# Strassen's seven products for blocks 6 to 17 of the Down products, in a decoder trunk on one Trainium2 core

## The chip, the core and the metric

The kernel runs on one core of one Trainium2 chip. The metric is the device time of one execution in microseconds; of several runs the median counts. Five engines work side by side, each with its own queue in fixed order: PE (TensorE, matmuls; its weight loads are listed as PEld), DVE (VectorE), ACT (ScalarE), POOL (GpSimd) and SP, which here only issues DMAs. POOL issues DMAs too, those that add what they load to what already lies in the tile.

## The reference

Two layers, each with two feed-forward parts around a mixer. Sequence 512, model width 1024, hidden width 2816 (22 blocks of 128), all in f32:

```python
def swiglu(x, w1, w3, w2):
    return (jax.nn.silu(x @ w1) * (x @ w3)) @ w2
...
    for l in range(DEPTH):
        h = x + 0.5 * swiglu(rms_norm(x, ffn1_norm[l]), ffn1_w1[l], ffn1_w3[l], ffn1_w2[l])
...
        h = h + y @ w_out[l]
        h = h + 0.5 * swiglu(rms_norm(h, ffn2_norm[l]), ffn2_w1[l], ffn2_w3[l], ffn2_w2[l])
        x = rms_norm(h, final_norm[l])
```

`x @ w1` and `x @ w3` are called Up here, the last product, with `w2`, Down. The mixer between the parts (convolution, window attention, attention to a memory) is not touched.

## The kernel before, in words

The activations lie transposed: h is [128, 8, 512], eight output blocks d of 128 channels by 512 positions. Each f32 product is made of three matmuls (mm3, lines 177 to 180): an operand is split into a high part that the matmul takes exactly and a low rest, and high x high, high x low and low x high are summed in PSUM. A split (line 145) is a copy on ACT that rounds (hi), then a subtraction on DVE (lo).

A feed-forward part (ffn, line 422) forms the hidden blocks f and folds them into h in four groups, QUARTERS (line 28): blocks 0 to 5, 6 to 11, 12 to 17, 18 to 21. Blocks 0 to 3 of Up are plain products, the others come in pairs from up_pair (line 358), by Strassen's seven products of quarters: two halves of the model width by two blocks, times two halves of the positions. Each of its seven units of weights (1024 columns, raw, a sum of raws, or X, which a load and an adding DMA on POOL's queue make, line 366) serves 24 matmuls of 256 columns. Their sums leave the four banks po and pt through ACT (part, lines 392 to 405) and DVE (add, line 386); then silu (line 414), the gating product (line 415) and the split of the gated blocks into ghi and glo (lines 416 to 419).

Behind a group's pairs, and one more pair made ahead for the next group, comes its Down (lines 488 to 506): for each of eight d a load of the group's columns of w2 into raw, one split, nf x 3 matmuls of 512 columns into one bank mm, and one update of h on DVE (line 506).

The order on each queue is set when the program is built: a scheduler with a model of the costs takes, for each engine, the earliest instruction in program order that its model has ready, and gives out the buffers in the same way; issue_after adds an edge. The chip then keeps that order. The buffers that matter: raw 3, aux (X) 3, whi and wlo 4 of 1024 columns each, ghi and glo 4 of two blocks each, g 2, u 1, part ("sq") 2, banks mm 3 and cf 1; mm() (line 86) takes cf every fourth time.

Of the kernel before, what the change touches and what calls it, by code (L numbers as in the profile page):

```python
# [10 lines left out]
F32 = mybir.dt.float32  # L11
F32R = mybir.dt.float32r
I32 = mybir.dt.int32
AF = mybir.ActivationFunctionType
# [4 lines left out]
P = 128  # L19
# [5 lines left out]
NT = S // P  # L25
FF = 2816
NF = FF // P
QUARTERS = ((0, 6), (6, 6), (12, 6), (18, 4))
CC = 3
TAPS = 31  # L30
PAD = TAPS - 1
# [34 lines left out]
def trunk(ctx: ExitStack, tc: tile.TileContext, xT, memT, pos, w1a, w3a, w2a, w1b, w3b, w2b,  # L66
# [19 lines left out]
    def mm():  # L86

        turn[0] += 1
        return bank([P, S], "mm" if turn[0] % 4 else "cf")
# [55 lines left out]
    def split(hi, lo, x, on):  # L145
        a = A.activation(hi, x, AF.Copy)  # L146
        return a, on.tensor_tensor(out=lo, in0=x, in1=hi.bitcast(F32), op=ALU.subtract)  # L147
# [34 lines left out]
    def at(p, *idx):  # L182
        return tuple(x[idx] for x in p)

    def blk(k, n=P):
        return slice(k * n, (k + 1) * n)
# [158 lines left out]
    def gated_pair():  # L345

        return (gp.tile([P, 2, S], F32R, tag="ghi", name="ghi"), gp.tile([P, 2, S], F32R, tag="glo", name="glo"))

    def gated():
        p = gated_pair()  # L350
        return [at(p, ALL, i, ALL) for i in range(2)]
# [6 lines left out]
    def up_pair(l, w13, f, M):  # L358
# [50 lines left out]
        for i in range(2):  # L409
            product(zv[i][:, x1], w, i, 4)  # L410
            add(to[i][:, 1, x0], zv[i][:, x1], part[i][:, x1])
        out = gated()
        for n, sign in enumerate((1.0, -1.0)):
            A.activation(u[:, n], u[:, n], AF.Silu, scale=sign)
        M.gated = V.tensor_tensor(out=g, in0=g, in1=u, op=ALU.mult)
        for n, sign in enumerate((1.0, -1.0)):
            hi, lo = out[n]
            A.activation(hi, g[:, n], AF.Copy, scale=sign)
            V.scalar_tensor_tensor(out=lo, in0=g[:, n], scalar=sign, in1=hi.bitcast(F32), op0=ALU.mult, op1=ALU.subtract)
        return out  # L420

    def ffn(l, w13, w2, x, sums, factors, last, at_product, aside=None, closing=None):

# [51 lines left out]
                    M.first()  # L475
        M.rest()
        hold.clear()
        for q, (f0, nf) in enumerate(QUARTERS):
            ahead = 2 if q + 1 < len(QUARTERS) else 0
            for f in range(f0, f0 + nf + ahead, 2):  # L480
                if f not in g:
                    g[f], g[f + 1] = up_pair(l, w13, f, M)
                    if f == PLAIN:
                        with tc.issue_after(M.gated.ins):
                            rescale = after()
            begun = []

            def begin(d):
# [770 lines left out]
```

## Time and profile before

| | us |
|---|---|
| median of three runs | 1771.48 (1764.68 to 1775.84) |
| the profiled execution | 1765.18, span 1763.4 |
| granted TensorE clock | 0.998 |

A page of the profile gives each engine's busy time over the span, the chain of waits that ended last, and groups of instructions by line, operation and shape. PE durations overlap, so the spacing of their starts says what a matmul costs.

### The profile page before, as it was taken

Reading aid. Unit: us, or ns where it says so; the run is one execution under the profiler, and the core shown is the slowest. Engines: PE = TensorE matmul, PEld = TensorE weight load, DVE = VectorE, ACT = ScalarE, POOL = GpSimd, SP = SyncE. Lnnn points to the kernel's source line nnn. Section 1 sums busy time; section 2 is a strip of 40 time slices with the busy share of each in tenths; the row PEclk is TensorE's granted clock in tenths of the full one; section 3 lists DMA queues with packets and bytes.
Section 4 is the critical chain, followed back from the end, with each engine's and each line's share of the span. In section 5 each row is a group of like instructions: output and inputs, shape, how many; then the busy total and the mean of one; then the engine's idle time right before and its main releaser. Section 6 shows DMA issues by size and latency. Waiting matters only on the chain.

```text
span 1763.4 us, 28084 instructions
## 1 busy us (share of the span) xinstructions
PE 1746.2 (99%) x11004; PEld 1575.8 (89%) x11004; DVE 1281.0 (73%) x1898; ACT 901.2 (51%) x1373; POOL 196.7 (11%) x220
## 2 busy tenths in 40 slices
PE   8999999999999999999999999999999999999998
PEld 6989999988888989898989898999888889998987
DVE  6969666589877857575678786666898777665756
ACT  6646444365765535353655453444567655353533
POOL 1001000016221000000010010000251310000000
PEclk9999999999999999999999999999999999999999
DMA  9556655267247546465566465642661666574622
GB/s 275 129 162 176 178 131 149 64 173 162 73 98 177 139 137 176 131 167 138 152 146 168 143 177 146 168 132 73 169 163 44 141 150 172 136 185 115 170 82 84
DMA packets 97205, 253.60 MB, mean 144 GB/s; under 512 B 9904, under 2 KB 16304, under 8 KB 97072
## 3 DMA queue, kind: packets, MB, share of 16 engines
q1 hardware_dynamic: 78064, 190.45, 35.6%
q0 software_dynamic: 19008, 61.35, 19.5%
q8 instruction: 86, 1.41, 0.3%
q14 instruction: 47, 0.39, 0.1%
HBM read 249.67 MB, written 2.10 MB: 143 GB/s over the span
## 4 chain that ended last, share of the span: by engine, by line
PE 89%; DVE 7%; DMA 2%; ACT 1%; issue 1%; SPq 0%; DVEq 0%; ACTq 0%
PE mm L178 13%; PE mm L179 12%; PE mm L180 12%; PE po L180 9%; PE po L178 9%; PE po L179 9%; PE pt L178 6%; PE pt L180 6%; PE pt L179 6%; DVE there L993 4%; PE po L870 1%; DMA raw<-in_wconv 1%; PE pt L859 1%; PE mm L818 1%; PE cf L178 0%
## 5 line engine op out<-in xcount | busy, mean ns | idle before, releaser
L146 ACT ACTIVATE whi<-raw 128x1024 fp32r<-128x1024 f32 (+3 forms) x346 | 326.1, 946 | 438.9 <-PE mm L179 222.6
L147 DVE TENSOR_TENSOR wlo<-raw,whi 128x1024 fp32r<-128x1024 f32 (+3 forms) x346 | 376.5, 1090 | 119.4 <-ACT whi L146 118.2
L179 PE MATMUL mm<-glo,whi 128*128 128x512 f32 (+1 forms) x752 | 292.3, 389 | 0.0
L178 PE MATMUL mm<-ghi,whi 128*128 128x512 f32 (+1 forms) x752 | 291.9, 390 | 0.0
L180 PE MATMUL mm<-ghi,wlo 128*128 128x512 f32 (+1 forms) x734 | 285.0, 388 | 0.0
L180 PE MATMUL po<-mh,wlo 128*128 128x256 f32 x864 | 244.7, 283 | 0.0
L179 PE MATMUL po<-ml,whi 128*128 128x256 f32 x864 | 244.7, 283 | 0.0
L178 PE MATMUL po<-mh,whi 128*128 128x256 f32 x864 | 244.6, 283 | 0.0
L180 PE MATMUL pt<-xhi,wlo 128*128 128x256 f32 x864 | 244.2, 283 | 0.0
L179 PE MATMUL pt<-xlo,whi 128*128 128x256 f32 x864 | 244.1, 283 | 0.0
L178 PE MATMUL pt<-xhi,whi 128*128 128x256 f32 x864 | 243.5, 283 | 0.0
L506 DVE SCALAR_TENSOR_TENSOR h<-mm,h 128x512 f32<-128x512 f32 x126 | 86.5, 689 | 129.5 <-PE mm L180 129.5
L178 PEld LDWEIGHTS mm<-ghi,whi 128*128 128x128 f32 x752 | 141.4, 188 | 28.8 <-DVE h L506 1.2
L179 PEld LDWEIGHTS pt<-xlo,whi 128*128 128x128 f32 x864 | 165.9, 192 | 0.8
L178 PEld LDWEIGHTS po<-mh,whi 128*128 128x128 f32 x864 | 165.9, 192 | 0.7
L179 PEld LDWEIGHTS po<-ml,whi 128*128 128x128 f32 x864 | 165.9, 192 | 0.6
L178 PEld LDWEIGHTS pt<-xhi,whi 128*128 128x128 f32 x864 | 165.3, 192 | 1.0
L179 PEld LDWEIGHTS mm<-glo,whi 128*128 128x128 f32 x752 | 141.4, 188 | 27.6
L180 PEld LDWEIGHTS po<-mh,wlo 128*128 128x128 f32 x864 | 165.9, 192 | 0.0
L180 PEld LDWEIGHTS pt<-xhi,wlo 128*128 128x128 f32 x864 | 165.8, 192 | 0.0
L180 PEld LDWEIGHTS mm<-ghi,wlo 128*128 128x128 f32 x734 | 137.9, 188 | 28.3
L993 DVE SCALAR_TENSOR_TENSOR there<-ypad,par,there 128x512 f32<-128x512 f32 x180 | 136.9, 784 | 1.1
(334 smaller groups left out, 3323.0 us busy)
## 6 DMA issues: line engine op xcount, KB each, us to landing
raw<-in_w2a SPq DMA_DIRECT2D x48, 384.0 KB, 3.6
raw<-in_w2b SPq DMA_DIRECT2D x48, 384.0 KB, 3.5
raw<-in_w1b SPq DMA_DIRECT2D x26, 512.0 KB, 3.6
raw<-in_w3b SPq DMA_DIRECT2D x26, 512.0 KB, 4.0
raw<-in_w1a SPq DMA_DIRECT2D x25, 512.0 KB, 3.7
raw<-in_w3a SPq DMA_DIRECT2D x25, 512.0 KB, 3.9
wsum<-in_w1a SPq DMA_DIRECT2D x18, 512.0 KB, 4.4
wsum<-in_w3a SPq DMA_DIRECT2D x18, 512.0 KB, 4.3
```

The costliest lines, as they stand in the source:

```text
L146: a = A.activation(hi, x, AF.Copy)
L147: return a, on.tensor_tensor(out=lo, in0=x, in1=hi.bitcast(F32), op=ALU.subtract)
L178: T.matmul(ps, a[0], b[0], start=first, stop=False, **more)
L179: T.matmul(ps, a[0], b[1], start=False, stop=False, **more)
L180: tail[0] = T.matmul(ps, a[1], b[0], start=False, stop=last, **more)
L506: added = V.scalar_tensor_tensor(out=h[:, d, :], in0=ps, scalar=0.5, in1=h[:, d, :], op0=ALU.mult, op1=ALU.add)
L818: tail[0] = T.matmul(pp[i][:, z, :], q, k, start=not masked, stop=True, skip_group_check=True)
L859: tail[0] = T.transpose(pt[:, i, j, :], pr[:, i, blk(j)], ident)
L870: tail[0] = T.matmul(po[:, 2 * c + i, :], ptb[:, i, j, :], v, start=(j == 0), stop=(j == nk - 1))
L993: V.scalar_tensor_tensor(out=cv[:, c, :], in0=ypad[:, c, j : j + S], scalar=conv_w[:, c, j : j + 1], in1=cv[:, c, :], op0=ALU.mult, op1=AL ...
```

## The change

GROUPS replaces QUARTERS: blocks 0 to 5 and 18 to 21 stay as they are, and 6 to 17 form three groups of four. For a group of four, down_four is called twice, for outputs 0 to 3 and 4 to 7. It takes the four blocks by four outputs of w2 and the four blocks by 512 positions of the gated values as two by two quarters, and forms seven products of quarters. A product is, for each of two outputs i, two blocks k by three matmuls of 256 columns.

The seven operands on the side of the gated values are made per pair in gated_parts: the split of the gated pair, four additions on POOL in place in g, and the split of the result into a second pair of ghi and glo. Since those four tiles then hold only one group, the gated pair made ahead waits in the list waiting, and gone() splits it when the next pair is about to be emitted.

The seven operands on the side of the weights are made in down_four: two loads of 1024 columns into raw, two sums xs on POOL in aux tiles (`xs[:, i]`), two additions in place on DVE per raw, and splits of 512 columns (half_unit). Sums of products leave PSUM through ACT into part and late, and reach h through POOL (most) or, straight from PSUM, through DVE (more, and one update over two outputs). late has the one buffer that is also u's.

The diff:

```diff
--- before.py
+++ after.py
@@ -25,7 +25,8 @@
 NT = S // P
 FF = 2816
 NF = FF // P
-QUARTERS = ((0, 6), (6, 6), (12, 6), (18, 4))
+GROUPS = ((0, 6), (6, 4), (10, 4), (14, 4), (18, 4))
+SEVEN = range(6, 18)
 CC = 3
 TAPS = 31
 PAD = TAPS - 1
@@ -409,15 +410,104 @@
         for i in range(2):
             product(zv[i][:, x1], w, i, 4)
             add(to[i][:, 1, x0], zv[i][:, x1], part[i][:, x1])
-        out = gated()
         for n, sign in enumerate((1.0, -1.0)):
             A.activation(u[:, n], u[:, n], AF.Silu, scale=sign)
         M.gated = V.tensor_tensor(out=g, in0=g, in1=u, op=ALU.mult)
+        return g
+
+    def split_gated(g):
+
+        out = gated()
         for n, sign in enumerate((1.0, -1.0)):
             hi, lo = out[n]
             A.activation(hi, g[:, n], AF.Copy, scale=sign)
             V.scalar_tensor_tensor(out=lo, in0=g[:, n], scalar=sign, in1=hi.bitcast(F32), op0=ALU.mult, op1=ALU.subtract)
         return out
+
+    T0, T1 = blk(0, QT), blk(1, QT)
+
+    def gated_parts(g, m):
+
+        plain = split_gated(g)
+        (a, b), (c, d) = (((g[:, n, T0]), g[:, n, T1]) for n in range(2))
+        G.tensor_tensor(out=d, in0=b, in1=d, op=ALU.add)
+        G.tensor_tensor(out=b, in0=a, in1=b, op=ALU.subtract)
+        G.tensor_tensor(out=a, in0=d, in1=a, op=ALU.subtract)
+        G.tensor_tensor(out=c, in0=a, in1=c, op=ALU.subtract)
+        p = gated_pair()
+        hi, lo = (x.rearrange("p n s -> p (n s)") for x in p)
+        split(hi, lo, g.rearrange("p n s -> p (n s)"), V)
+        sums = [at(p, ALL, i, ALL) for i in range(2)]
+        for j, z, n, t in ((1, plain, 0, T0), (2, plain, 1, T0), (3, plain, 1, T1), (6, sums, 0, T0), (5, sums, 0, T1), (4, sums, 1, T0), (7, sums, 1, T1)):
+            m.setdefault(j, []).append(at(z[n], ALL, t))
+
+    def down_four(l, w2, f0, d0, m):
+
+        xs = wst.tile([P, UNIT], F32, tag="aux", name="wsum", bufs=3).rearrange("p (i n k c) -> p i n k c", i=2, n=2, k=2)
+        raw, rows = [], []
+        for i in range(2):
+            r = wst.tile([P, UNIT], F32, tag="raw", name="raw", bufs=3)
+            d = d0 + 2 * i
+            nc.sync.dma_start(r.rearrange("p (d c) -> p d c", d=2), w2[l, d : d + 2, :, f0 * P : f0 * P + 512].rearrange("d p c -> p d c"))
+            v = r.rearrange("p (d k s c) -> p d k s c", d=2, k=2, s=2)
+            raw.append(r[:, 0:512])
+            rows.append(v)
+            G.tensor_tensor(out=xs[:, i], in0=v[:, :, :, 0], in1=v[:, 1].rearrange("p k s c -> p s k c"), op=ALU.add)
+        banks = [mm() for _ in range(4)]
+        xy, zv = banks[:2], banks[2:]
+        part = [tm("part", "sq", 2) for _ in range(2)]
+        late = tmp.tile([P, 2, S], F32, tag="u", name="late", bufs=1)
+
+        def half_unit(x):
+            p = at(pair(), ALL, slice(0, 512))
+            split(p[0], p[1], x, V)
+            return p
+
+        def product(ps, w, block, j, first=False):
+            for k in range(2):
+                mm3(ps, at(w, ALL, blk(block(k))), m[j][k], first and not k, k == 1, skip_group_check=True)
+
+        def more(d, t, ps):
+            V.scalar_tensor_tensor(out=h[:, d, t], in0=ps, scalar=0.5, in1=h[:, d, t], op0=ALU.mult, op1=ALU.add)
+
+        def most(d, t, x, op=ALU.add):
+            G.tensor_tensor(out=h[:, d, t], in0=h[:, d, t], in1=x, op=op)
+
+        for i in range(2):
+            d = d0 + 2 * i
+            w = half_unit(raw[i])
+            product(xy[i][:, T0], w, lambda k: 2 * k, 1, first=True)
+            product(xy[i][:, T1], w, lambda k: 2 * k + 1, 2)
+            A.activation(part[i], xy[i], AF.Copy, scale=0.5)
+            most(d, T0, part[i][:, T0])
+            most(d, T0, part[i][:, T1])
+            v = rows[i][:, 0]
+            V.tensor_tensor(out=v[:, :, 0], in0=v[:, :, 0], in1=xs[:, i, 1], op=ALU.add)
+            V.tensor_tensor(out=v[:, :, 1], in0=v[:, :, 1], in1=v[:, :, 0], op=ALU.add)
+        for i in range(2):
+            w = half_unit(raw[i])
+            product(xy[i][:, T0], w, lambda k: 2 * k, 6)
+            A.activation(late[:, i, T0], xy[i][:, T0], AF.Copy, scale=0.5)
+            product(zv[i][:, T0], w, lambda k: 2 * k + 1, 3, first=True)
+        for i in range(2):
+            d = d0 + 2 * i
+            w = half_unit(xs[:, i].rearrange("p n k c -> p (n k c)"))
+            product(xy[i][:, T0], w, lambda k: 2 + k, 5)
+            A.activation(late[:, i, T1], xy[i][:, T0], AF.Copy, scale=0.5)
+            product(zv[i][:, T1], w, lambda k: k, 7)
+            V.scalar_tensor_tensor(out=h[:, d : d + 2, T1], in0=zv[i].rearrange("p (n t) -> p n t", n=2), scalar=0.5, in1=h[:, d : d + 2, T1],
+                                   op0=ALU.mult, op1=ALU.add)
+            most(d, T1, late[:, i, T1])
+            most(d + 1, T1, late[:, i, T1], ALU.subtract)
+        w = at(pair(), ALL, slice(0, 512))
+        for i in range(2):
+            hi, lo = (x[:, blk(i, QT)].rearrange("p (k c) -> p k c", k=2) for x in w)
+            split(hi, lo, rows[i][:, 1, :, 1], V)
+        for i in range(2):
+            d = d0 + 2 * i
+            product(zv[i][:, T1], w, lambda k: 2 * i + k, 4)
+            more(d + 1, T0, zv[i][:, T1])
+            most(d + 1, T0, late[:, i, T0], ALU.subtract)
 
     def ffn(l, w13, w2, x, sums, factors, last, at_product, aside=None, closing=None):
 
@@ -475,14 +565,33 @@
                     M.first()
         M.rest()
         hold.clear()
-        for q, (f0, nf) in enumerate(QUARTERS):
-            ahead = 2 if q + 1 < len(QUARTERS) else 0
+        waiting, parts, done = [], {}, set(g)
+
+        def gone():
+
+            while waiting:
+                f, z = waiting.pop(0)
+                if f in SEVEN:
+                    gated_parts(z, parts.setdefault((f - 6) // 4, {}))
+                else:
+                    g[f], g[f + 1] = split_gated(z)
+
+        for q, (f0, nf) in enumerate(GROUPS):
+            ahead = 2 if q + 1 < len(GROUPS) else 0
             for f in range(f0, f0 + nf + ahead, 2):
-                if f not in g:
-                    g[f], g[f + 1] = up_pair(l, w13, f, M)
+                if f not in done:
+                    gone()
+                    waiting.append((f, up_pair(l, w13, f, M)))
+                    done.add(f)
                     if f == PLAIN:
                         with tc.issue_after(M.gated.ins):
                             rescale = after()
+            if f0 in SEVEN:
+                for d in (0, 4):
+                    down_four(l, w2, f0, d, parts[q - 1])
+                continue
+            if not ahead:
+                gone()
             begun = []
 
             def begin(d):
```

## The prediction

> **What bounds the kernel now.** I read the page first: its engines, and the chain that ended last.
>
> ```profile
> span 1763.4 us, 28084 instructions
> PE 1746.2 (99%) x11004; PEld 1575.8 (89%) x11004; DVE 1281.0 (73%) x1898; ACT 901.2 (51%) x1373; POOL 196.7 (11%) x220
> PE 89%; DVE 7%; DMA 2%; ACT 1%; issue 1%; SPq 0%; DVEq 0%; ACTq 0%
> ```
>
> TensorE is never without work, and 89% of the chain is its matmuls. Then the windows of one group of the second feed-forward part: three pairs of Up, then the Down products of six blocks.
>
> ```profile
> 651.60:712.10 60.50, 60.50 (x500) 60.22 (x499) 41.51 (x52) 33.32 (x48) 5.18 (x6) 1.00 0.70 178
> 712.10:744.70 32.60, 32.60 (x151) 27.24 (x150) 19.71 (x25) 9.11 (x11) 0.00 (x0) 1.00 0.37 107
> ```
>
> After the window come us, then PE, PEld, DVE, ACT and POOL busy, the clock, the DMA share and GB/s. PE fills both windows, at full clock. So nothing can be won there but matmul time, and every stall that the change brings counts in full. DVE is busy for 69% of Up and 60% of Down; POOL adds nothing in Down. The waits of that Down window say how the splits are placed:
>
> ```profile
> ACT whi L146 <- PE mm L179: 19.2, 7, 3.2
> DVE h L506 <- PE mm L180: 10.5, 7, 2.5
> ```
>
> ACT waits for PE to give a weight buffer back: the splits run ahead of PE as far as four buffers allow.
>
> **The matmuls.** How long a matmul holds PE is read from starts, since the durations overlap. First a run of 256 columns, then the first of a run of 132 of 512 columns and the matmul that follows its last:
>
> ```profile
> 599.72 0.28 PE L180 MATMUL po<-mh,wlo 128*128 128x256 f32 x1
> ...
> 601.52 0.28 PE L180 MATMUL po<-mh,wlo 128*128 128x256 f32 x1
> ...
> 714.84 0.40 PE L178 MATMUL mm<-ghi,whi 128*128 128x512 f32 x1
> ...
> 744.79 0.28 PE L178 MATMUL po<-mh,whi 128*128 128x256 f32 x1
> ```
>
> Between the first two lie 15 starts: 1.80 / 15 = 0.120 us. The others give 29.95 / 132 = 0.227 us. Four blocks times four outputs are 4 x 4 x 3 = 48 matmuls of 512 columns now, 48 x 0.227 = 10.90 us. Seven products of 2 x 2 x 3 are 84 of 256 columns, 84 x 0.120 = 10.08 us. The eighth product saves 12.5% of the columns, but half a matmul costs 0.120 and not 0.1135, so 0.82 us is left. Down_four is called 3 x 2 times in each of four parts: 24 x 0.82 = **19.7 us saved**. That is all the change can win: PE has no idle time in Down to give back.
>
> **What it puts on DVE and ACT.** The spacing of back-to-back DVE instructions:
>
> ```profile
> 666.33 0.68 DVE L386 TENSOR_TENSOR u<-pt,part 128x512 f32<-128x512 f32 x1
> 666.93 0.68 DVE L386 TENSOR_TENSOR raw<-raw 128x512 f32<-128x512 f32 x1
> ...
> 676.70 1.22 DVE L147 TENSOR_TENSOR wlo<-wsum,whi 128x1024 fp32r<-128x1024 f32 x1
> 677.84 0.42 DVE L386 TENSOR_TENSOR u<-part 128x256 f32<-128x256 f32 x1
> 678.17 1.29 DVE L419 SCALAR_TENSOR_TENSOR glo<-g,ghi 128x512 fp32r<-128x512 f32 x2
> ```
>
> That is 0.60 us for 512 elements, 1.14 for 1024 and 0.33 for 256. One down_four holds six splits of 512 and two of 256 (4.26), four adds into raw of 256 (1.32), and out of PSUM two updates of 512 and two of 256 (1.86): 7.4 us in 10.1 us of PE, of which 5.6 have both inputs in SBUF. A pair of blocks adds one split of 1024 (1.14). By itself DVE would still keep up, 74% busy where it was 60%.
>
> ```profile
> L146 ACT ACTIVATE whi<-raw 128x512 fp32r<-128x512 f32 x36 | 21.8, 625 | 29.8 <-issue 16.6 <-PE pt L179 8.3 <-DMA raw<-in_w2b 2.3
> L400 ACT ACTIVATE part<-po 128x256 f32<-128x256 f32 x72 | 27.3, 380 | 71.1 <-PE po L180 70.9 <-PE pt L179 0.2
> ```
>
> ACT gets six copies of 512 and two of 256 for the splits, two of 512 for part, four of 256 for late: 8 x 0.62 + 6 x 0.38 = 7.2 us of 10.1. I take nothing for it; its cover is the 2.9 us left over in each call, and if that is gone, PE waits for the difference.
>
> **What it puts on POOL.** The trace has no add of 256 elements there, but one of 512, and products of 64 and 192:
>
> ```profile
> L1018 POOL TENSOR_TENSOR aux<-there x2: 1256/1258/1259, 480.6 to 1352.3; 128x512 f32<-128x512 f32 x2
> L753 POOL TENSOR_TENSOR uu<-query,sg x32: 320/874/2593, 398.1 to 1292.3; 128x192 f32<-128x192 f32 x16, 128x64 f32<-128x64 f32 x16
> ```
>
> From 0.320 (the shortest, 64) and 1.258 (512) an element costs (1258 - 320) / 448 = 2.1 ns, so 256 take an estimated 0.72 us; the bounds are 0.54 (its elements alone) and 1.26. A down_four has two adds of 512 and ten of 256, 9.7 us; a pair of blocks has four of 256, 2.9 us. A cycle of two pairs and two down_fours (60.5 us of PE) gets 25.2 us of POOL, and 12 cycles 302 us. POOL has the room; two other things do not.
>
> First, **POOL's adds stop DVE**:
>
> ```profile
> 403.33 1.40 DVE L993 SCALAR_TENSOR_TENSOR there<-ypad,par,there 128x512 f32<-128x512 f32 x2
> ...
> 479.88 2.58 DVE L993 SCALAR_TENSOR_TENSOR there<-ypad,par,there 128x512 f32<-128x512 f32 x2
> ...
> 480.65 1.26 POOL L1018 TENSOR_TENSOR aux<-there 128x512 f32<-128x512 f32 x1
> ...
> 400.67 0.67 DVE L584 TENSOR_REDUCE hs<-hsq 128x8 f32<-128x512 f32 x1
> 398.05 3.16 POOL L753 TENSOR_TENSOR uu<-query,sg 128x192 f32<-128x192 f32 x4 [2.51 <-ACT query L748]
> ```
>
> Two taps in a row take 1.40 us, and 2.58 beside one POOL add of 1.26: DVE loses 1.18 us, nearly the whole add. The one-input reduction at 400.67 takes its usual 0.67 beside POOL. So a DVE instruction with two SBUF inputs and a POOL add take turns. (The page "SBUF — State Buffer" of the Trainium skill, section "Who interferes with whom", has the same two halves and makes the lock last the whole instruction, with the second comer blocked. By that rule an add of 256 would cost DVE all of its duration; the third rival below works that out.)
>
> Two down_fours (20.2 us of PE) have 14.9 us of DVE's own. Twenty adds of 256 and three of 512 fall among them (the first call's first is early): 20 x 0.54 + 3 x 1.18 = 14.3 us by the elements alone, 17.9 by the estimated 0.72 of the whole add; I take 16, the middle. If DVE always found work behind an add, it would need 14.9 + 16 = 31 us; if never, 14.9. DVE's two-input share is 75%, and I estimate that it has work behind four adds of five, so I take 60%: 14.9 + 9.6 = 24.5, 4.3 us more than PE needs. Of the four weight buffers three lie ahead of PE, 3 x 12 matmuls x 0.120 = 4.3 us, less 1.2 for a split itself: 3.1 us are covered. **1.2 us of stall** a cycle (bounds 0 and 7.7). In Up the same share leaves DVE room: three pairs and the Down between them show 41.51 + 19.71 = 61.2 us of 93.1.
>
> Second, **the order of POOL's queue**. The second call's weights in xs come from two adds of 512 behind the first call's ten; DVE's adds into raw and ACT's copy stand behind them. Its second raw tile needs a third buffer that the first call frees with its last split, and a load:
>
> ```profile
> raw<-in_w2a SPq DMA_DIRECT2D x48, 384.0 KB, 3.6
> raw<-in_w1a SPq DMA_DIRECT2D x25, 512.0 KB, 3.7
> ```
>
> I follow the adds with 1.1 us each beside a busy DVE: the first call's first four end at 6.4 us after its start, the next four (behind the second half's updates) at 12.3, its last two at 14.5. The sum of the second xs then ends at 16.1, two DVE adds and a copy later, each a little held up, the operand is there at 17.9, and PE, unhindered, is at its products 3 x 1.44 us into the second call, at 14.4: 3.5 us late. Put ahead of the last six adds it is in time. Late has one buffer, in turn with u of Up, so the next call's late and the next pair's u also wait for those last adds. Between 0 and 3.5 I take **2.0 us** a cycle.
>
> Queued behind the waits: in POOL's queue the accumulating loads of the next pair of Up (two per pair); in ACT's and DVE's queues, behind gated_parts' four adds, the next splits. In Up three buffers of 24 matmuls lie ahead, 8.6 us, against 2.9 of adds: nothing taken; without that cover, up to 2.9 us a pair. SP's loads keep their bytes. The gating of the pair made ahead moves behind both down_fours, since its two pairs of operand tiles come free there: two copies of 0.62 on ACT, 1.2 + 1.14 us on DVE and four POOL adds fall into the next pair's 20.2 us, and only the pair after that (g has two buffers) waits for them. I take nothing; if POOL's lag reached that far, the lag itself would be the price, as in the second rival.
>
> **The sum.** The profiled execution took 1765.2 us. 1765.2 - 19.7 + 12 x (1.2 + 2.0) = 1783.9. The median of the runs shown is 6.3 us above that execution, so I say 1771.5 + 18.7 = **1790 us**, about 1.1% slower.
>
> **The rivals.** *The cover holds*: the scheduler puts POOL's adds into DVE's waits and its PSUM updates, and the xs sums early. DVE's 26% of free time in Down speaks for it, the one buffer of late against. Fully held it gives 1771.5 - 19.7 = 1752. It decides from the point where a cycle stalls less than 19.7 / 12 = 1.6 us; half held, 0.8 a cycle, 1761.
>
> *DVE and POOL run one after the other*: both have work whenever the other has, each call lasts as long as their sum, and late and u hand POOL's lag on to the next pair. A cycle then stalls 31 - 20.2 - 3.1 = 7.7 us, or some 5 if partly: 1771.5 - 19.7 + 60 = 1812, up to 1844. The four POOL products at 398.05, taking turns with taps, speak for it; DVE's waits for PE in Down speak against.
>
> *Every add blocks for its whole duration*: the twenty adds of 256 take 0.72 each from DVE, 17.9 instead of 16 a cycle, and 60% of the difference is 1.1 us a cycle more: 1804. The 1.18 lost of 1.26 at 479.88 speaks for it, the 0.320 us of the shortest product, too little to be seen beside a tap, says nothing. (That is the rule of "SBUF — State Buffer" named above, in the section "Who interferes with whom".)
>
> **How the numbers follow.** The forecast (1.7 to 5 us a cycle, 1772 to 1812) has 0.40, and a little over half of it lies within 1%. The cover fully held (under 1754) has 0.08, half held (1754 to 1772) 0.19, the whole add 0.09, one after the other (over 1812) 0.24. One per cent, 17.7 us, is about what a measurement of this kernel tells from no change. So faster 0.08, same 0.19 + 0.22 = 0.41, slower 0.18 + 0.09 + 0.24 = 0.51. From 1753 to 1838 leaves out 0.07 below and about 0.12 above; the forecast's own range is 1772 to 1812.
>
> **What would show it.** Right: Down matmuls of 256 columns 0.120 us apart; POOL near 500 us and DVE near 1400 busy; adds of 256 on POOL above 0.72 us at the mean; DVE splits of 512 in Down well above 0.69; PE gaps in Down that end with a split, mostly in the second call of each cycle. Wrong: a PE without gaps in Down (the cover holds); gaps that end on DMA or an ACT queue, or lie in Up; splits that take 0.69 beside POOL's adds.

## The result and the profile after

The changed kernel takes 1899.92 us at the median of four runs (1897.42 to 1912.06), the kernel before, on the same chip, 1768.08 (1764.24 to 1775.84): a ratio of 1.0753, 95% interval 1.0691 to 1.0815. Slower, as forecast, but by 132 us and not by 19; the time lies 62 us above the end of the range.

The page of the changed kernel's profiled execution (1897.42 us): span, busy time by engine, and the chain that ended last by engine.

```profile
span 1895.6 us, 30982 instructions
PE 1784.5 (94%) x11868; PEld 1637.9 (86%) x11868; DVE 1548.8 (82%) x2178; ACT 1020.4 (54%) x1669; POOL 602.7 (32%) x604
PE 67%; DVE 15%; DMA 8%; issue 4%; ACT 4%; POOL 1%; ACTq 0%; DVEq 0%; SPq 0%; POOLq 0%
```

PE's part of the chain fell from 89% to 67%, DVE's doubled. What PE waits for (us in total, times, longest); the kernel before had none of these:

```profile
PE po L181 <- DVE wlo L148: 31.3, 14, 4.8
PE mm L179 <- ACT whi L147: 27.0, 15, 3.3
PE mm L181 <- DVE wlo L148: 15.6, 11, 3.3
```

PE waits for operands: for the low part that DVE makes, and for ACT's copy. po is Up, mm the four-block Down: both halves of a cycle are hit. In Down one place stands out. Of the 15 waits for ACT's copy 12, one in each cycle and 21.7 of the 27.0 us, stand behind a load of w2 into raw: the second raw tile of a cycle's second call, whose buffer the first call frees with its last splits. One such case, from DVE's split that frees the buffer over load, copy and subtraction to PE's two waits:

```profile
734.35 0.96 DVE L148 TENSOR_TENSOR wlo<-raw,whi 128x256 fp32r<-128x256 f32 x1
735.34 0.37 SPq L451 DMA_DIRECT2D raw<-in_w2b  x1
740.57 0.63 ACT L147 ACTIVATE whi<-raw 128x512 fp32r<-128x512 f32 x1 [2.98 <-DMA raw<-in_w2b]
741.23 4.24 DVE L148 TENSOR_TENSOR wlo<-raw,whi 128x512 fp32r<-128x512 f32 x1 [2.11 <-ACT whi L147]
741.25 0.39 PE L179 MATMUL mm<-ghi,whi 128*128 128x256 f32 x1 [1.21 <-ACT whi L147]
745.53 0.58 PE L181 MATMUL mm<-ghi,wlo 128*128 128x256 f32 x1 [3.25 <-DVE wlo L148]
```

The windows of one cycle, its Down and then its Up, and two short ones inside the next Up:

```profile
730.17:757.20 27.03, 21.32 (x158) 20.27 (x156) 23.07 (x29) 12.62 (x28) 18.17 (x19) 0.94 0.46 136
757.20:802.48 45.28, 41.74 (x326) 41.53 (x327) 39.66 (x42) 24.42 (x35) 16.41 (x17) 0.92 0.49 123
833.00:838.00 5.00, 0.21 (x2) 0.00 (x1) 5.00 (x2) 0.60 (x1) 4.92 (x7) 0.96 0.65 107
838.00:841.20 3.20, 3.19 (x15) 3.19 (x16) 3.17 (x4) 1.75 (x2) 0.54 (x1) 0.53 0.02 5
```

The third: PE idle for 5 us while DVE and POOL are both busy throughout. The fourth: when PE starts again, the granted clock is 0.53. The matmuls there:

```profile
832.93 0.28 PE L180 MATMUL po<-ml,whi 128*128 128x256 f32 x1
838.01 0.58 PE L181 MATMUL po<-mh,wlo 128*128 128x256 f32 x1 [4.80 <-DVE wlo L148]
838.39 0.42 PE L179 MATMUL po<-mh,whi 128*128 128x256 f32 x1
...
840.95 0.30 PE L179 MATMUL po<-mh,whi 128*128 128x256 f32 x1
```

From 838.39 to 840.95 lie 12 starts: 0.213 us each, where 0.120 is usual. (The Trainium skill, "TensorE: Matmul & The Clock Gate", Part 1, says that after an idle window of about 3.4 us the array runs at 1.2 GHz, half its clock, until it has been busy for about as long. The trace agrees here: 3.2 us at 0.53 behind 5 us of standstill. It also shows half the clock behind less: 3.4 us at 0.50 from 1284.7 us on, behind one idle time of 2.79 us.)

**Where the 132 us are.** For every matmul of 256 or 512 columns I took the spacing to the next start beyond 0.120 or 0.227. Before, stalls of this kind come to 17.0 us; after, to 132.5, of them 64.8 in the four-block Down, 49.8 in Up, 17.9 elsewhere, about as before. Some 49 of Down's 64.8 us stand at the 12 matmuls, of a cycle's 168, that need the late raw tile. Spacings near 0.21 behind a stall come to 3.8 us before (43 matmuls) and 41.8 after (441). So 24 x 0.82 = 19.7 us of matmul time went, 115.5 of stalls and 38.0 of slow clock came: +133.8, against 132.2 between the spans.

### The profile page after: what moved, and what is told of

Read it like the earlier page. It is cut to its first block, busy times and chain, and to the rows that moved or that the text cites. A ratio compares the mean times of both kernels' runs of the same rounds, so it can differ in the third digit from the quotient of the medians.

```text
span 1895.6 us, 30982 instructions
## 1 busy us (share of the span) xinstructions
PE 1784.5 (94%) x11868; PEld 1637.9 (86%) x11868; DVE 1548.8 (82%) x2178; ACT 1020.4 (54%) x1669; POOL 602.7 (32%) x604
## 4 chain that ended last, share of the span: by engine, by line
PE 67%; DVE 15%; DMA 8%; issue 4%; ACT 4%; POOL 1%; ACTq 0%; DVEq 0%; SPq 0%; POOLq 0%
PE mm L181 9%; PE mm L179 9%; PE mm L180 8%; DVE wlo L148 8%; PE po L181 7%; PE po L179 7%; PE po L180 7%; PE pt L179 5%; PE pt L181 5%; PE pt L180 5%; DMA raw<-in_w2b 2%; ACT whi L147 2%; DVE there L1102 2%; DMA raw<-in_w2a 1%; PE po L979 1%
## 5 line engine op out<-in xcount | busy, mean ns | idle before, releaser
L148 DVE TENSOR_TENSOR wlo<-raw,whi 128x1024 fp32r<-128x1024 f32 (+3 forms) x426 | 473.3, 1121 | 134.5 <-ACT whi L147 133.4
L147 ACT ACTIVATE whi<-raw 128x1024 fp32r<-128x1024 f32 (+3 forms) x426 | 347.9, 828 | 409.8 <-DVE raw L387 86.9
L179 PE MATMUL mm<-ghi,whi 128*128 128x256 f32 (+1 forms) x896 | 303.8, 341 | 30.4 <-ACT whi L147 27.0
L181 PE MATMUL mm<-ghi,wlo 128*128 128x256 f32 (+1 forms) x878 | 292.6, 337 | 16.2 <-DVE wlo L148 15.6
L180 PE MATMUL mm<-glo,whi 128*128 128x256 f32 (+1 forms) x896 | 299.4, 334 | 0.0
L179 PEld LDWEIGHTS mm<-ghi,whi 128*128 128x128 f32 x896 | 178.5, 199 | 52.4 <-ACT whi L147 32.2
L181 PEld LDWEIGHTS mm<-ghi,wlo 128*128 128x128 f32 x878 | 173.8, 200 | 33.8 <-DVE wlo L148 20.0
L180 PEld LDWEIGHTS mm<-glo,whi 128*128 128x128 f32 x896 | 178.4, 199 | 13.5
L474 POOL TENSOR_TENSOR h<-h,late 128x256 f32<-128x256 f32 x144 | 143.7, 1093 | 53.0 <-ACT late L496 31.4
L148 DVE TENSOR_TENSOR wlo<-wsum,whi 128x1024 fp32r<-128x1024 f32 (+1 forms) x120 | 147.8, 1254 | 6.5 <-ACT whi L147 6.5
```

The costliest lines, as they stand in the source:

```text
L179: T.matmul(ps, a[0], b[0], start=first, stop=False, **more)
L180: T.matmul(ps, a[0], b[1], start=False, stop=False, **more)
L181: tail[0] = T.matmul(ps, a[1], b[0], start=False, stop=last, **more)
L474: G.tensor_tensor(out=h[:, d, t], in0=h[:, d, t], in1=x, op=op)
```

## The experiments

First theory, *contention*: POOL's additions read SBUF, and DVE's subtractions with two SBUF inputs lose time beside them. Rivals: *order* (operands and buffers come late through POOL's queue and its waits), *load* (DVE has too much work of its own), and *grouping* (four blocks at a time costs something by itself).

**plain_fours: the groups of four with plain Down products.**

```diff
-SEVEN = range(6, 18)
+SEVEN = range(0)
```

> Keeps the groups of four blocks, but forms their Down products plainly (SEVEN is empty), so nothing of the seven products is left. Port theory (POOL's adds hold DVE's second read path, DVE's splits come late, PE stalls and its clock falls): as before, 1768 within 8 us. Grouping theory (the shorter groups and the later gating of the pair made ahead cost the time): over 1800 us. The seven products themselves would then cost the rest.

1766.39, ratio 0.9978 (0.9959 to 0.9996). Grouping falls; everything comes from the seven products.

**write_only: every POOL addition becomes two memsets of the same length, which read nothing.**

```diff
-            G.tensor_tensor(out=h[:, d, t], in0=h[:, d, t], in1=x, op=op)
+            for _ in range(2):
+                G.memset(x, 0.0)
```

and likewise for the four additions in g and the one into xs. The result is no longer the reference's.

> Every one of POOL's adds of the change becomes two memsets that write as many elements and read nothing (the h updates through part and late, the sums of the gated values and xs are left out, so the output is not the reference's). The waits for part and late, their single buffers and POOL's place in the order stay. Port theory: DVE is no longer held up; DVE splits of 512 back at 0.69 us, PE without stalls and at full clock, 1750 to 1775 us. Order theory (waits for late, u and for what is queued on POOL): still over 1830 us. Load theory (DVE's and ACT's own extra instructions are too many): still over 1850 us.

1766.72, ratio 0.9989 (0.9972 to 1.0007): all 132 us are gone. DVE's groups (count, busy us and mean ns, idle before) in the changed kernel, then in write_only:

```profile
L148 DVE TENSOR_TENSOR wlo<-raw,whi 128x512 fp32r<-128x512 f32 x132 | 121.3, 928 | 61.8 <-ACT whi L147 61.8
L148 DVE TENSOR_TENSOR wlo<-wsum,whi 128x512 fp32r<-128x512 f32 x48 | 53.5, 1151 | 0.4 <-ACT whi L147 0.4
L485 DVE TENSOR_TENSOR raw<-raw,wsum 128x256 f32<-128x256 f32 x48 | 38.2, 796 | 2.1
L498 DVE SCALAR_TENSOR_TENSOR h<-mm,h 128x512 f32<-128x512 f32 x24 | 16.3, 679 | 0.5 <-PE mm L181 0.4
```

```profile
L148 DVE TENSOR_TENSOR wlo<-raw,whi 128x512 fp32r<-128x512 f32 x132 | 89.3, 686 | 42.8 <-ACT whi L147 42.7
L148 DVE TENSOR_TENSOR wlo<-wsum,whi 128x512 fp32r<-128x512 f32 x48 | 30.9, 685 | 0.0
L491 DVE TENSOR_TENSOR raw<-raw,wsum 128x256 f32<-128x256 f32 x48 | 20.2, 421 | 0.8
L504 DVE SCALAR_TENSOR_TENSOR h<-mm,h 128x512 f32<-128x512 f32 x24 | 16.6, 691 | 12.0 <-PE mm L181 11.9
```

Beside additions a subtraction of 512 takes 0.93 to 1.15 us, beside memsets 0.69; the update whose input lies in PSUM takes 0.68 to 0.69 in both. Write_only's page:

```profile
span 1769.6 us, 31368 instructions
PE 1736.4 (98%) x11868; PEld 1605.0 (91%) x11868; DVE 1393.8 (79%) x2178; ACT 1022.0 (58%) x1669; POOL 422.0 (24%) x988
```

The same 2178 DVE instructions take 1548.8 - 1393.8 = 155.0 us more in the changed kernel, 0.40 for each of POOL's 384 additions. One limit: memsets also hold POOL for less (422 us against 603), so its queue runs earlier here too, and as they leave h alone, none waits for DVE's updates of it. And though nothing is lost to contention, write_only isn't 19.7 us faster: 15.9 us of stalls stand in Up, which holds more DVE and ACT work than before.

**no_h_adds and h_adds_on_dve: the 240 additions into h left out, or on DVE.**

```diff
-            G.tensor_tensor(out=h[:, d, t], in0=h[:, d, t], in1=x, op=op)
+            return
```

```diff
-            G.tensor_tensor(out=h[:, d, t], in0=h[:, d, t], in1=x, op=op)
+            V.tensor_tensor(out=h[:, d, t], in0=h[:, d, t], in1=x, op=op)
```

> Leaves out the 240 POOL adds into h alone (the output lacks their terms); the 48 sums xs and the 96 sums of gated values stay on POOL. Port theory: the lock time on POOL falls from some 270 us to some 110 us and its trains lose most of their length, so more than half of the 132 us goes: 1775 to 1815 us. Order theory: late and part come free without POOL, so all of it goes: under 1765 us. Load theory: over 1850 us.

> The 240 adds into h go from POOL to DVE (0.33 us each, 10 in a down_four). DVE then has 7.4 + 3.3 = 10.7 us of its own in each 10.1 us of PE, but 240 fewer POOL adds stand in its way. Port theory: faster than the changed kernel by 60 us or more, 1790 to 1830 us, and DVE the bound in Down. Load theory: slower than the changed kernel, over 1920 us.

1820.20, ratio 1.0277 (1.0244 to 1.0310), and 1863.09, ratio 1.0523 (1.0486 to 1.0559). Both are above what I expected of contention, the first by 5 and the second by 33 us. They speak against the rivals too: order had the first under 1765, load had it over 1850 and the second over 1920. And they say this: DVE doing the 240 additions itself costs 43 us (1863 against 1820), POOL doing them 80 (1900 against 1820).

**all_on_dve: all 384 additions on DVE.** As above, with the other five lines from G to V.

> All 384 POOL adds of the change go to DVE; nothing of the change reads SBUF on POOL any more. DVE's own work in a down_four is 7.4 + 3.3 + 1.2 = 11.9 us against 10.1 of PE, and 1.3 more a pair in Up. Port theory: although DVE has more to do than with the h adds alone moved (1863 us), it is faster, 1800 to 1845 us, by DVE's overload in Down (24 x 1.8 = 43 us) and some loss of clock. Load theory: slower than 1863, about 1890.

1831.85, ratio 1.0374 (1.0347 to 1.0401), as expected. From its page:

```profile
PE 1760.5 (96%) x11868; PEld 1613.9 (88%) x11868; DVE 1524.2 (83%) x2562; ACT 1022.6 (56%) x1669; POOL 197.4 (11%) x220
```

DVE does all the additions itself in 1524.2 - 1393.8 = 130 us of its time; shared with POOL, they cost it 155. And without contention and without POOL's queue 65 us of loss remain, so DVE's own load counts as well. Two attempts to make that load less, **lean_xs** (the first two products straight from PSUM by DVE, xs by a copy and two accumulating loads) and **lean** (the low part of unchanged operands by ACT and an accumulating load too):

```diff
-            G.tensor_tensor(out=xs[:, i], in0=v[:, :, :, 0], in1=v[:, 1].rearrange("p k s c -> p s k c"), op=ALU.add)
+            A.activation(xs[:, i], v[:, :, :, 0], AF.Copy)
+            for n in range(2):
+                G.dma_start(xs[:, i, n], w2[...][:, n], accum_op=ALU.add)
```

> As all_on_dve, but M1 and M2 reach h straight from PSUM on DVE without part, and xs is made by a copy on ACT and two accumulating DMAs. No POOL add, 10.7 us of DVE in a down_four (7.4 + 10 x 0.33), 10.1 of PE. Port theory: 1775 to 1800 us. If POOL's DMA issues (six more a call) hold DVE up too: over 1850.

> As lean_xs, and the low part of the two unchanged weight units of a call is made by ACT and an accumulating DMA as elsewhere in the kernel, so DVE has 9.5 us in a down_four against 10.1 of PE. Port theory: the first version in which DVE fits, 1755 to 1780 us; below 1766 it beats the kernel before. If the later low parts (a DMA of its own on POOL's queue behind others) keep PE waiting: over 1790.

1876.82, ratio 1.0623 (1.0585 to 1.0661), and 1927.44, ratio 1.0902 (1.0873 to 1.0930). Misses: in lean_xs PE waited 48.9 us for ACT's copy of raw, most of it behind DVE's additions into raw, which waited 45.0 us for the loads into xs; in lean PE waited 66.3 us for the loads into wlo. Accumulating loads come too late in steps this short; they settle nothing on DVE.

**probe and probe_apart: contention by itself.** Two small kernels that hold nothing of the model: 24 DVE subtractions of 512, and beside them POOL additions, memsets or loads.

```python
lambda: (two(24), adds(8)),
lambda: (two(24), load(), adds(8)),
lambda: (one(24), load(), adds(8)),
```

In probe all additions write one tile, so that each waits for the one before; in probe_apart each has a tile of its own.

> A kernel of its own that computes nothing of the reference: between barriers, DVE subtracts 512 elements with both inputs in SBUF (or takes one input from PSUM), beside POOL's adds of 256 or 512, with or without an accumulating DMA issued on POOL just before, or beside POOL's memsets. Turn-taking (what the prediction assumed): each POOL add costs DVE its 0.54 to 0.72 us, no subtraction lasts over 1.4 us, with or without the DMA. Train theory: adds that stand ready in POOL's queue behind a DMA follow one another every 0.68 us and hand the read path on among themselves, so one subtraction lasts as long as all eight, 5 us or more; without the DMA they take turns. Both: nothing is lost beside memsets, the DMA alone, or with an input from PSUM.

> The probe again, with an output tile of its own for every instruction, so that no instruction has to wait for the one before it on its own engine. If that is what let DVE in between in the first probe: adds that stand ready follow one another every 0.68 us without a gap, and one DVE subtraction lasts as long as the train of eight, 5 us and more, with a DMA in front or without. If a DMA in front is needed: only in the steps with the DMA. If they take turns whatever stands in front: no subtraction over 1.9 us, and the long waits of the changed kernel need another cause.

Of probe_apart, additions on POOL alone (start, us, count at the end), and then three windows (us; DVE, ACT and POOL busy with counts): eight additions beside subtractions, the same behind an accumulating load's issue, and that with DVE's input in PSUM:

```profile
19.54 4.12 POOL L39 TENSOR_TENSOR pz<-pa,pb 128x256 f32<-128x256 f32 x6
```

```profile
23.85:32.98 9.13, 9.13 (x9) 0.00 (x0) 9.13 (x8) 1.00 0.00 0
43.65:49.39 5.74, 5.74 (x1) 0.00 (x0) 5.73 (x9) 1.00 0.59 93
83.31:89.08 5.77, 5.77 (x11) 0.00 (x0) 5.77 (x9) 1.00 0.57 91
```

Alone an addition takes 4.12 / 6 = 0.69 us. Beside subtractions the two take turns: 8 additions and some 8 subtractions in 9.13 us, 1.14 each, so each side loses over 0.4. Behind a load's issue the eight follow each other in a *train* of 5.74 us, and one subtraction stands for all of it. With DVE's input in PSUM, DVE loses nothing. In probe, where additions wait for each other, no train forms. The changed kernel has such trains (the one beside the 5 us gap, POOL and DVE):

```profile
831.83 0.89 POOL L367 DMA_DIRECT2D wsum<-in_w1b  x1
832.44 2.40 POOL L474 TENSOR_TENSOR h<-h,late 128x256 f32<-128x256 f32 x3
834.50 1.02 POOL L434 TENSOR_TENSOR g<-g 128x256 f32<-128x256 f32 x1
835.18 1.01 POOL L474 TENSOR_TENSOR h<-h,late 128x256 f32<-128x256 f32 x1
835.86 1.00 POOL L435 TENSOR_TENSOR g<-g 128x256 f32<-128x256 f32 x1
```

```profile
832.37 5.58 DVE L148 TENSOR_TENSOR wlo<-raw,whi 128x1024 fp32r<-128x1024 f32 x1 [1.08 <-ACT whi L147]
```

Ten DVE instructions with SBUF inputs stand for over 4 us beside such rows of additions. That gave a second theory, *trains*, against *turn-taking* (0.4 us an addition, wherever it falls).

**one_by_one and chain_gh: no trains, the same work.** An edge makes each POOL addition into h, in chain_gh each into h or g, wait for the one before it to have ended.

```diff
+    def one_by_one(this):
+        if previous:
+            tc.add_manual_dep(this.ins, previous.pop().name, ...)
+        previous.append(this.ins)
...
-            G.tensor_tensor(out=h[:, d, t], in0=h[:, d, t], in1=x, op=op)
+            one_by_one(G.tensor_tensor(out=h[:, d, t], in0=h[:, d, t], in1=x, op=op))
```

> The changed kernel with one thing more: each of the 240 POOL additions into h waits for the one before it to have ended; which instructions run, and on which engine, stays. Trains (POOL additions that follow one another every 0.68 us behind a DMA issue, while a DVE subtraction stands for 4 to 6 us): they can't form, so DVE's subtractions lose one or two additions at most, PE's waits for wlo of 4 to 5 us go, and with them much of the slow clock: 1835 to 1880. Turn-taking alone (each addition costs DVE about 0.4 us wherever it falls, 384 of them): the same sum of stalls, 1890 to 1910. Load of DVE alone (it has too little slack in the four-block steps for anything): 1890 to 1920, with PE's waits as long as before.

> The changed kernel, with each of POOL's 336 additions of 256 (into h and into g) waiting for the one before it to have ended. In the run one_by_one only those into h waited; additions into g went between them, so that a wait was always met already, and five DVE instructions still stood for 4 to 6 us (12 in the changed kernel). Here no train can form: no DVE instruction that reads SBUF should last over 3 us beside POOL's additions. Trains theory: PE's stalls of 3 us and more go and with them the slow clock behind them, 1840 to 1875. Turn-taking theory (the 384 additions cost DVE some 0.4 us each, trains or not): 1880 to 1910. Order of POOL's queue (the additions into g now stand behind all those into h): over 1910, with PE waiting for ghi or glo.

1894.07, ratio 1.0703 (1.0670 to 1.0736), and 1897.99, ratio 1.0739 (1.0708 to 1.0770). In one_by_one two such instructions of 4.8 us were left, as additions into g went between those into h. (The "five" and "12" in the expectation of chain_gh counted waits on semaphores too; of instructions that compute, two and ten lasted over 4 us.) In chain_gh the longest lasts 2.6. Its page, and two groups of its subtractions:

```profile
span 1896.3 us, 31099 instructions
PE 1791.5 (94%) x11868; PEld 1636.0 (86%) x11868; DVE 1545.7 (82%) x2178; ACT 1019.6 (54%) x1669; POOL 626.9 (33%) x604
```

```profile
L148 DVE TENSOR_TENSOR wlo<-raw,whi 128x512 fp32r<-128x512 f32 x132 | 114.6, 878 | 63.1 <-ACT whi L147 63.1
L148 DVE TENSOR_TENSOR wlo<-wsum,whi 128x512 fp32r<-128x512 f32 x48 | 56.2, 1208 | 0.4 <-ACT whi L147 0.4
```

The trains are gone, DVE's busy time is within 3.1 us of the changed kernel's, and the time is the same. My second theory falls: a train bundles the loss and makes it visible, but the sum counts. The rival of order gets no support either: here the additions into g stand behind all those into h, and nothing moves.

**two_halves and two_halves_dve: twice as many operands ahead.** The operands of 512 columns of i = 0 and 1 share one buffer, of which each took a whole one and used half; in the changed kernel, and in all_on_dve.

```diff
-        def half_unit(x):
-            p = at(pair(), ALL, slice(0, 512))
+        def half_unit(x, i):
+            if not i:
+                both[:] = pair()
+            p = at(both, ALL, slice(512 * i, 512 * i + 512))
             split(p[0], p[1], x, V)
             return p
```

> The changed kernel with one thing other: the operands of 512 columns of outputs i = 0 and 1 share one weight buffer of 1024 columns (before, each took a whole buffer and used half), so that four buffers hold eight such operands and up to six or seven lie ahead of PE in Down instead of three. All work stays where it is. Cover theory (DVE's lost time turns into PE stalls in Down because three operands, 4.3 us, are too little): the stalls in the four-block Down, 65 us of gaps and 23 of slow clock, fall by half or more: 1830 to 1870. Latency or rate theory (the operands are late because DVE, ACT and POOL make them one after the other, however many buffers there are): 1885 to 1910. Lumps (a buffer comes free only when both halves are used): over 1910.

> As all_on_dve (all 384 additions on DVE, no add on POOL; 1831.85), with the shared weight buffers of two_halves. Cover theory: its 33 us of gaps and 9 of slow clock in the four-block Down fall by half or more, 1795 to 1815. Latency or rate theory: 1825 to 1840. Lumps: over 1840.

1864.45, ratio 1.0536 (1.0510 to 1.0562), and 1800.17, ratio 1.0169 (1.0137 to 1.0201). The totals are those of the cover theory, but the place isn't. Stalls in Up fell from 49.8 to 27.8 and (all_on_dve) from 34.0 to 7.0; those in the four-block Down stayed, 64.8 to 63.4 and 33.2 to 32.7. Running ahead in Down lets DVE and ACT reach the next Up sooner; Down itself stays bound by how fast its operands are made. In two_halves no wait of PE in Down stands behind a load of w2 any more, against 37.3 us in the changed kernel (21.7 for the copy and 15.6 for the subtraction behind it). In their place come waits for other low parts and 16.5 us for updates of h, both DVE's work:

```profile
PE cf L181 <- DVE wlo L148: 19.5, 12, 2.3
PE mm L179 <- DVE h L502: 13.7, 7, 2.2
PE cf L179 <- DVE h L502: 2.8, 4, 1.3
```

In two_halves_dve PE waits there for ACT's copy into late:

```profile
PE mm L179 <- ACT late L494: 26.8, 12, 3.6
```

**no_late_dve: two_halves_dve without the tile late.**

```diff
-            A.activation(late[:, i, T0], xy[i][:, T0], AF.Copy, scale=0.5)
+            more(d0 + 2 * i + 1, T0, xy[i][:, T0], -0.5)
...
-            A.activation(late[:, i, T1], xy[i][:, T0], AF.Copy, scale=0.5)
+            more(d, T1, xy[i][:, T0])
+            more(d + 1, T1, xy[i][:, T0], -0.5)
```

> two_halves_dve without the tile late: the sums that went through it (four ACT copies of 256 and six DVE additions a call) reach h straight from PSUM in six DVE updates of 256. In two_halves_dve 26.8 us of PE's waits are for ACT's copy into late, whose one buffer is also u's. If that buffer is the rest of the loss, these waits go and nothing of the kind takes their place: 1762 to 1780. If DVE is simply at its limit there (1517 us busy, 92% in the four-block steps), the waits move to wlo, whi or h: 1790 to 1810.

1807.98, ratio 1.0223 (1.0207 to 1.0238). The wait changes its name and stays:

```profile
PE mm L179 <- DVE h L474: 34.0, 25, 3.8
```

The one buffer of late wasn't the rest of the loss: PE now waits for DVE's updates.

**Half the dose: half_pool, half_dve, half_shared, half_no_late.** Seven products for outputs 0 to 3 alone, plain ones for 4 to 7; additions on POOL, on DVE, on DVE with shared buffers, and that without late.

```diff
-                for d in (0, 4):
-                    down_four(l, w2, f0, d, parts[q - 1])
-                continue
+                down_four(l, w2, f0, 0, parts[q - 1])
...
-            for d in range(KD if ahead or not closing else KD - 2):
+            for d in range(4 if f0 in SEVEN else 0, KD if ahead or not closing else KD - 2):
```

> As half_dve, but with the adds on POOL as in the changed kernel. Port theory: DVE has less of its own (7.4 + 4.8 = 12.2 of 21.0 us), yet it is slower than half_dve; stalls in the seven half remain, 1785 to 1830 us. Load theory: faster than half_dve, under 1760.

> The seven products only for outputs 0 to 3 of each group of four blocks, outputs 4 to 7 plainly behind them, and all adds of the change on DVE. PE saves 12 x 0.82 = 9.8 us. DVE has 11.9 + 4 x 1.2 = 16.7 us in 21.0 of a group's Down and some 17.7 in the 20.2 us of a pair. Port and load theories together: DVE fits now and POOL reads nothing, so 1755 to 1768 us, as fast as before or a little faster. If the seven products need more lead than the plain ones whatever the load: over 1785.

> half_dve (seven products for outputs 0 to 3 alone, all additions on DVE; 1765.48) with the weight buffers shared as in two_halves. half_dve has 4.8 us of gaps in Up beyond those of the kernel before and 1 in the four-block steps; the shared buffers took 27 us from Up in two_halves_dve. Cover theory: 1758 to 1763. Nothing left to cover: 1763 to 1768.

> half_shared without the tile late, as in no_late_dve. With half the seven products DVE has room for all of it, so nothing of PE's 9.8 us should be lost any more: 1756 to 1762. If the gaps left have another cause (the Up pairs themselves): as half_shared, within 2 us.

| | us | ratio (95% interval) | stalls, us | DVE busy, us |
|---|---|---|---|---|
| half_pool | 1802.48 | 1.0197 (1.0174 to 1.0220) | 53.5 | 1464.8 |
| half_dve | 1765.48 | 0.9987 (0.9965 to 1.0009) | 23.9 | 1435.2 |
| half_shared | 1760.26 | 0.9954 (0.9942 to 0.9966) | 19.5 | 1437.4 |
| half_no_late | 1770.77 | 1.0009 (0.9997 to 1.0020) | 29.6 | 1435.9 |

With half the dose, no addition on POOL and shared buffers the stalls are nearly those of before (17.0), and 8.0 of the 12 x 0.82 = 9.8 us saved are left: half_shared is the one version of the seven products whose interval lies wholly below the kernel before, by 0.46%. One more thing differs in these runs: with one call a group, no copy on ACT waits for down_four's loads of w2 (12 do in the changed kernel), so they don't tell less work on DVE from the missing late raw tile. Leaving late out was a miss: PE's next product now waits for DVE (7.8 us at the update of h) instead of ACT.

## Why the prediction was wrong

**The saving** was right. Write_only's windows of the same cycle, which have the changed kernel's matmuls without its contention:

```profile
697.44:716.04 18.60, 18.60 (x157) 18.60 (x156) 15.38 (x28) 12.06 (x26) 9.71 (x34) 1.00 0.60 180
716.04:756.48 40.44, 39.38 (x329) 39.17 (x328) 33.67 (x45) 24.50 (x35) 11.84 (x34) 1.00 0.61 153
```

In Down PE has no gap, and 18.60 / 155 starts are 0.120 us.

**The mechanism** was right: two-input subtractions lose beside POOL's additions, updates from PSUM don't. The size of the loss was nearly right where it was looked for: DVE's busy time in Down rises from 15.38 to 23.07, 7.7 us a cycle, where the text took 9.6 (60% of 16). The whole-instruction rule, the third rival, is too dear: an addition of 0.72 costs DVE 0.40.

**The step that failed** is the one that follows: "Of the four weight buffers three lie ahead of PE [...] 3.1 us are covered. **1.2 us of stall** a cycle". The excess that it starts from was nearly right, in part by luck: in these windows DVE has 23.07 us of work where PE has 18.60, 4.5 more, and the text has 4.3; less was lost beside POOL than it took, but 13 of the 168 matmuls run earlier, among those of Up, and leave PE less here. Nothing of the excess was covered: Down grows by 27.03 - 18.60 = 8.4 us (1.7 of it slow clock), the 4.5 and the 4.0 us in which DVE is idle there. Nor was DVE's idle time the room that 14.9 us of its own against 20.2 of PE suggests: DVE is idle for 3.2 us of that Down without contention and for 4.0 with it. Over the whole span idle time is 1769.6 - 1393.8 = 375.8 against 1895.6 - 1548.8 = 346.8: of the 155 us lost, 29 came out of it and 126 out of the span, slow clock included. What DVE waits for, first in write_only, then in the changed kernel:

```profile
DVE wlo L148 <- ACT whi L147: 130.6, 139, 4.7
```

```profile
DVE wlo L148 <- ACT whi L147: 139.9, 117, 4.4
```

Where most of Down's stalls stand, at the second call's second raw tile, the cover was 0.6 us and not 3.1. A weight buffer can be filled ahead only when the raw tile is there. Write_only, the same cycle as above:

```profile
701.13 0.37 SPq L455 DMA_DIRECT2D raw<-in_w2b  x1
705.62 1.15 ACT L147 ACTIVATE whi<-raw 128x512 fp32r<-128x512 f32 x2 [0.75 <-DMA raw<-in_w2b]
707.16 0.28 PE L179 MATMUL mm<-ghi,whi 128*128 128x256 f32 x1
```

Without contention, too, ACT's copy starts 0.08 us after the load lands, in all 12 cycles, and ends at the mean 0.6 us before PE needs it. With POOL's additions DVE comes later to the split that frees the buffer: the load is issued 11.5 us after the cycle's first Down matmul where it was 8.5, takes 5.4 us where it took 4.5, and the subtraction behind the copy takes 2.3 us where it took 0.7 (means of 12). PE stands still. So DVE's idle time there is a wait inside a chain (last split on DVE, load, copy on ACT, subtraction on DVE, matmul), not room.

The late tile carries the loss, but it doesn't set its size: in two_halves, where PE no longer waits behind it, Down's stalls are 63.4 us as before. My reading is that three operands ahead, or six, cover a single delay, while a rate that is too low empties them and then comes out in full. That is argued from these rows; a fourth buffer for raw was not tried, and no run made the chain shorter with DVE's work kept.

**"Nothing taken" for Up** was the second failure. The four additions in g and the last ones into h fall into Up: DVE is busy there for 39.66 us where write_only shows 33.67, and Up takes 45.28 instead of 40.44: 4.8 us a cycle, of which 2.2 are slow clock. The price named for the case without cover, up to 2.9 us for each of a cycle's two pairs, holds it; the value taken was 0.

**The clock** was missing from the sum: 38.0 us, a quarter of what was lost, and none of the terms or rivals has it. That stalls cause it is argued from their order and from the runs. In the changed kernel's trace half the clock comes 17 times before the kernel's last few us, for 3.4 or 6.8 us each, and every time behind 1.8 us or more of PE idle in the 6.8 us before; the kernel before has it at its end alone. And slow matmuls rise with stalls: 43 with 17.0 us of stalls (before), 117 with 53.5 (half_pool), 269 with 69.9 (no_h_adds), 441 with 132.5 (changed).

**"The order of POOL's queue"**, 2.0 us a cycle, was worked out for the operand from xs, and there it shows nowhere: DVE has 0.4 us of idle time before its 48 splits, PE hardly waits for it, and chain_gh, with another order, takes the same time. But the same paragraph names the second call's second raw tile, with the buffer that the first call's last split frees, and a load. It puts no price on it. That tile is where some 49 us of stalls stand, 4.1 a cycle, behind a late split on DVE and not behind an addition that waits its turn on POOL.

In numbers: foreseen -19.7 + 12 x 3.2; measured -19.7 + 115.5 + 38.0. Of the rivals, "one after the other" came nearest (5 to 7.7 us a cycle in Down), and its forecast was also too low, as it counted neither Up nor the clock. Of the marks named beforehand, the spacing, gaps mostly in a cycle's second call, DVE's longer splits and POOL's longer additions came; the last in the changed kernel:

```profile
L474 POOL TENSOR_TENSOR h<-h,late 128x256 f32<-128x256 f32 x144 | 143.7, 1093 | 53.0 <-ACT late L496 31.4 <-DVE h L498 11.1 <-DVE h L471 10.6
```

POOL was busier than foreseen (603 against 500), DVE too (1549 against 1400, which write_only's 1394 meets); and gaps in Up, named as a sign against, came as well, as did gaps behind a copy that had waited for a DMA.

Open: how the 65 us of all_on_dve divide between the amount of DVE's work, the order in which it takes it, and the late raw tile, at which some 20 of its 33.2 us of stalls in Down stand. half_shared, at 1437 us of DVE, stalls little more than the kernel before, two_halves_dve, at 1517, for 57.3 us; they differ in more than DVE's work.

## What to carry to other kernels

Where PE is busy for 99%, count a loss on the engine that feeds it almost in full (126 of 155 us here), unless the trace shows that engine's idle time to be free and not a wait in the same chain. Before you count buffers as cover, follow the operand that comes last back through its copy to its load, and to what frees the load's buffer. Work moved to POOL isn't free for DVE: 384 additions cost it 155 us there, and 130 where it did them itself. And a stall of some microseconds on PE is paid with a surcharge, here 38.0 us of slow clock on 115.5 of stalls.

## What the runs showed of the hardware

Turn-taking: a DVE subtraction of 512 with both inputs in SBUF takes 1.14 us beside POOL additions and 0.69 alone; beside POOL memsets it takes 0.69 too, and an update of 512 with its input in PSUM 0.68 beside additions. (The Trainium skill, "SBUF — State Buffer", section "Who interferes with whom", has which instructions contend; that whoever issues first blocks the other for its whole instruction doesn't tell that waiting sides alternate, as here.) New to me was the train: behind the issue of an accumulating load, POOL additions that don't wait for each other run on for 5.74 us and keep one subtraction waiting all that time, while without the load the same additions alternate with DVE.
